# A two-layer decoder trunk on one Trainium2 core: a running sum moved into PSUM, a mask moved to VectorE, and a new order of the work

## The chip, the core and the metric

The kernel runs on one core of a Trainium2 chip. The core has four engines that compute: TensorE (PE in the profile; the loading of its stationary operand is shown apart, as PEld), VectorE (DVE), ScalarE (ACT) and GpSimd (POOL). SyncE (SP) only starts transfers. Each engine runs its own instructions in the order in which they were written, and waits on semaphores for the others. SBUF is the working memory of 128 partitions, PSUM the memory that TensorE writes to, in banks of 512 f32 columns.

The metric is the time of one execution on the device in microseconds, lower is better. A time of a kernel is the median of its runs.

## What is computed

Two layers with 256 positions and 1024 channels. Each layer runs four sub-layers, each between two RMS norms:

```
x += 0.5 * post(swiglu(pre(x)))     # FFN, 2816 hidden channels
x +=       post(mixer(pre(x)))      # layer 0: mLSTM, layer 1: attention
x += 0.5 * post(swiglu(pre(x)))     # second FFN
x +=       post((p @ w_ple) * sigmoid(pre(x) @ w_gate))
```

In the attention of layer 1 there are 8 heads with two score matrices each; a score matrix is masked so that a query sees no later key, its row maximum is subtracted, and the exponentials are summed:

```
s = q @ k.T;  s = where(key_pos <= query_pos, s, -inf);  a = softmax(s)
diff = a[:, :, 0] - lam * a[:, :, 1];  o = diff @ v
```

## The kernel before

**Tiles.** The 256 positions are two tiles of 128 (t is 0 or 1). A product with f32 accuracy is made of three TensorE passes: every operand is split into a rounded part (`whi`, `xh`, `hh`: ScalarE copies it) and the rest (`wlo`, `xl`, `hl`: VectorE subtracts), and hi·hi, hi·lo and lo·hi are added in PSUM (`mm3`, line 610). So each weight block of 128 partitions x 2048 columns passes through a DMA into a `wraw` buffer, a 2048-wide ScalarE copy and a 2048-wide VectorE subtraction before TensorE can use it.

**PSUM.** There are three banks `accI` for products with input weights, four `accO` for the sums of the output projections and one `tr` for transposes.

**Block pairs.** Two neighbouring blocks of 512 FFN columns are computed together (`block_pair`, line 821) by a scheme that takes seven products of half blocks where eight would do it plainly. A product is 12 matmuls of 512 columns (`times`, line 866). The scheme needs sums and differences of weights (`wraw` + `wraw`, made by VectorE, or by a DMA that adds, which POOL starts) and of inputs (`forms`, line 803). Its first lines are the ones that change:

```
ax, ay = acc_in(), acc_in()
times(ax, quarter(0, 0), w11, False)
p1 = held(ax)                                     # ScalarE copies the bank to SBUF
times(ay, quarter(0, 4), w21, False)
nc.vector.tensor_tensor(p1, ay, p1, op=ALU.add)   # VectorE adds the two products
use(0, 0, p1)
```

After these lines `ax` goes on being summed up by the next product of the scheme, so the copy `p1` is needed. The FFNs have 19 block pairs, the mLSTM two more. `hidden` (line 921) takes the result `p1` through SiLU and a multiplication and transposes it for the output projection (`stage_out`, line 940).

**End of a sub-layer.** `post` (line 703) takes the squares of the sum (ScalarE), adds them (POOL), takes the power of -0.5 (POOL), and VectorE adds the scaled result to `x`. `pre` (line 785) transposes `x` on TensorE in two halves, multiplies by a gain (VectorE, `att<-tr,gcol`) and splits the result into `xh` (ScalarE) and `xl` (VectorE), the inputs of the next products.

**Attention.** `weights` (line 1349) puts the mask into two PSUM banks with a matmul (identity times a mask tile, line 1355), adds the scores onto it with matmuls of 64 rows, and VectorE takes the maximum of a whole bank (line 1368). ScalarE then takes the exponentials from PSUM.

**The last step.** `ple` (line 1044) ends the kernel: for the second tile it works on pieces of 512, 256 and 256 columns, takes the squares of each on ScalarE, adds three sums on POOL, and takes the power.

**The order of the work.** No instruction stands where the code writes it. `trunk` only records operations; a planner (`Notes.play`, line 350) plays them through with a cost for each (`cost`, line 258) and for transfers (`step`, `later`, lines 400 to 414), picks at each moment an operation for an engine that is free, and so sets the order of each engine and the buffers. TensorE takes the ready operation of lowest rank, the others the one that is due first (`backward`, line 311). Three tables written out by hand then bend the plan: `FIRST` (this operation before that), `SHIFT` (change when an operation is due) and `MOVE` (change the rank of matmuls). `SLACK` and `LATE` are times added to the landing of an adding and of a plain transfer. What the planner thinks of costs has no part in the run: only the order it writes does.

Of the kernel before, what the change touches and what calls it, by code (L numbers as in the profile page):

```python
# [33 lines left out]
)  # L34
SHIFT = (
# [16 lines left out]
)  # L52
MOVE = (
# [12 lines left out]
)  # L66
SLACK = 3000
LATE = 1000
LANES = 8
# [15 lines left out]
LOCAL = {(0, 0, 3)}  # L85

# [1541 lines left out]
```

## Time and profile before

| what | value |
|---|---|
| median of 3 runs | 991.07 us (989.76 to 994.2) |
| the profiled execution's own time | 990.61 us |
| its span, first to last instruction | 988.8 us |
| TensorE busy | 977.0 us, 99% of the span |
| VectorE busy | 896.0 us, 91% |
| ScalarE busy | 714.7 us, 72% |
| GpSimd busy | 99.7 us, 10% |
| transfers | 274.70 MB, mean 278 GB/s |

A row of the timeline gives the start, the duration, the engine, the operation as `out<-in` with buffer numbers left out, its shape, a count, and in brackets the idle time of that engine just before and what ended it. Matmuls overlap one another, so the pace of TensorE is read from the distance of starts and not from durations. A row of the waits gives who waited for whom, the sum, the number of times and the longest. All lines read L536 in before, because one line writes out every recorded operation; groups are told apart by tiles.

### The profile page before, as it was taken

The page shows a single profiled execution, that of the slowest core. Times are in us where ns is not written, and L with a number is a line of the kernel's source. Part 1 is how long each engine was busy: PE and PEld are TensorE (multiplying, and loading weights), DVE is VectorE, ACT ScalarE, POOL GpSimd, SP SyncE. Part 2 cuts the span into 40 slices and gives each one's busy share as a digit, 9 for nine tenths or more (in the row PEclk, how much of TensorE's full clock was granted, in tenths as well). Part 3 has the DMA queues.
Part 4 walks back from the last instruction along what each step waited for, and adds up shares of the span by engine and source line. Part 5 has one row for each costly group of instructions (what it writes and reads, how often), then busy time and mean ns, then how long its engine had stood idle before and what let it go on. Part 6 is the DMA issues. An engine that isn't in the chain of part 4 may idle for free. (4 is left out here: it accounts for less than half of the span.)

```text
span 988.8 us, 12411 instructions
## 1 busy us (share of the span) xinstructions
PE 977.0 (99%) x4598; PEld 798.9 (81%) x4598; DVE 896.0 (91%) x898; ACT 714.7 (72%) x954; POOL 99.7 (10%) x133
## 2 busy tenths in 40 slices
PE   9999999999999999999999999999999999999997
PEld 7878888887777888888888888888888888888886
DVE  6999999789999999998799999898975999999983
ACT  7668767678867776776777777686775777867763
POOL 0000000300140000001120000001102320000010
PEclk9999999999999999999999999999999999999999
DMA  9999956966799999775699999854668799995721
GB/s 356 414 313 350 286 218 256 304 215 221 288 312 296 328 339 318 292 272 205 258 299 336 334 353 350 325 217 192 216 253 259 214 340 346 305 287 229 284 86 43
DMA packets 45862, 274.70 MB, mean 278 GB/s; under 512 B 5481, under 2 KB 5865, under 8 KB 16105
## 3 DMA queue, kind: packets, MB, share of 16 engines
q1 hardware_dynamic: 39752, 231.69, 60.1%
q0 software_dynamic: 5760, 41.95, 20.9%
q8 instruction: 36, 0.59, 0.2%
q10 hardware_dynamic: 288, 0.27, 0.1%
q14 instruction: 26, 0.20, 0.1%
HBM read 263.40 MB, written 10.49 MB: 277 GB/s over the span
## 5 line engine op out<-in xcount | busy, mean ns | idle before, releaser
L536 DVE TENSOR_TENSOR wraw<-wraw,wraw 128x2048 f32<-128x2048 f32 x44 | 100.5, 2283 | 0.1
L536 ACT ACTIVATE whi_0r<-wraw 128x2048 fp32r<-128x2048 f32 (+2 forms) x49 | 79.5, 1633 | 12.7 <-DVE wraw L536 4.7
L536 ACT ACTIVATE whi_2r<-wraw 128x2048 fp32r<-128x2048 f32 (+1 forms) x49 | 77.8, 1599 | 12.5 <-PE accI L536 8.1
L536 ACT ACTIVATE whi_1r<-wraw 128x2048 fp32r<-128x2048 f32 (+2 forms) x50 | 77.7, 1567 | 8.4 <-DVE wraw L536 4.0
L536 ACT ACTIVATE att<-accI 128x512 f32<-128x512 f32 x84 | 49.7, 593 | 44.6 <-PE accI L536 44.0
L536 ACT ACTIVATE whi_3r<-wraw 128x2048 fp32r<-128x2048 f32 (+1 forms) x46 | 74.2, 1616 | 10.4 <-PE accI L536 4.4
L536 ACT ACTIVATE whi_5r<-wraw 128x2048 fp32r<-128x2048 f32 (+1 forms) x46 | 77.3, 1688 | 5.9 <-PE accI L536 3.3
L536 ACT ACTIVATE whi_4r<-wraw 128x2048 fp32r<-128x2048 f32 (+1 forms) x45 | 73.5, 1645 | 8.3 <-PE accI L536 5.2
L536 POOL DMA_DIRECT2D wraw<-in_ffn_in x36 | 32.0, 889 | 335.2 <-DMA wraw<-in_ffn_in 203.6
L536 POOL TENSOR_SCALAR sm<-sm 128x1 f32<-128x1 f32 x32 | 29.1, 909 | 287.2 <-ACT sg L536 281.7
L536 ACT ACTIVATE sg<-att,sm 128x256 f32<-128x256 f32 x57 | 28.4, 502 | 18.7 <-DVE att L536 17.9
L536 POOL TENSOR_TENSOR sm<-sm,mhalf 128x1 f32<-128x1 f32 (+2 forms) x40 | 28.9, 722 | 101.5 <-DVE sm L536 98.9
L536 ACT ACTIVATE sg<-accO 128x512 bf16<-128x512 f32 (+2 forms) x46 | 20.4, 450 | 21.2 <-PE accO L536 15.6
L536 PEld LDWEIGHTS tr<-ident,sg 128*128 128x128 f32 x176 | 23.4, 140 | 13.4 <-DVE hl_0r L536 1.7
L536 PE MATMUL tr<-ident,sg 128*128 128x128 f32 x176 | 33.8, 273 | 0.1
L536 DVE SCALAR_TENSOR_TENSOR wraw<-wraw,sm,wraw 128x512 f32<-128x512 f32 x32 | 22.6, 748 | 10.4 <-POOL sm L536 10.4
L536 DVE TENSOR_TENSOR wlo_0r<-wraw,whi_1r 128x2048 fp32r<-128x2048 f32 (+1 forms) x13 | 25.3, 1955 | 3.8 <-PE accI L536 3.5
L536 DVE TENSOR_TENSOR att<-accI,att 128x512 f32<-128x512 f32 x42 | 28.3, 682 | 0.0
L536 ACT ACTIVATE att<-accI,sm 128x512 f32<-128x512 f32 (+1 forms) x22 | 14.7, 668 | 17.2 <-PE accI L536 17.1
L536 DVE SCALAR_TENSOR_TENSOR sg<-att,sm,sg 128x256 f32<-128x256 f32 x57 | 26.8, 479 | 0.1
L536 ACT ACTIVATE hh_2r<-tr 128x256 fp32r<-128x256 f32 x30 | 11.3, 378 | 21.2 <-PE tr L536 10.1
L536 DVE TENSOR_TENSOR wlo_2r<-wraw,whi_0r 128x2048 fp32r<-128x2048 f32 (+1 forms) x12 | 25.2, 2108 | 1.4 <-ACT whi_0r L536 1.1
(610 smaller groups left out, 3242.5 us busy)
## 6 DMA issues: line engine op xcount, KB each, us to landing
wraw<-in_ffn_in SPq DMA_DIRECT2D x102, 1024.0 KB, 8.8
wraw<-in_ffn_out SPq DMA_DIRECT2D x44, 1024.0 KB, 10.1
wraw<-in_ffn_in POOLq DMA_DIRECT2D x36, 1024.0 KB, 13.4
wraw<-in_mlstm_in SPq DMA_DIRECT2D x14, 1024.0 KB, 6.4
wraw<-in_ple_gate SPq DMA_DIRECT2D x8, 1024.0 KB, 5.5
wraw<-in_w_kv SPq DMA_DIRECT2D x8, 1024.0 KB, 4.9
home<-wraw SPq DMA_DIRECT2D x28, 256.0 KB, 3.5
wraw<-home SPq DMA_DIRECT2D x14, 512.0 KB, 4.4
```

Of the source, the lines that this page charges most:

```text
L536: getattr(getattr(self.nc, eng), name)(*args, **kw)
```

## The change

Four things are changed, in code that also gets options which stay off here (`PAIRED` is empty, `cut` is never used).

First, in 16 block pairs (four of each of the four FFNs; a pair that an FFN begins with is left as it was) ScalarE copies the first product from one PSUM bank to another, and the second product is added onto that copy by TensorE. VectorE's addition goes away, and the result is read from PSUM.

Second, in attention the mask matmuls go. VectorE adds the mask and takes the minimum of the negated sums in one operation for each score tile (128 or 256 columns), writes the tile to SBUF, and ScalarE takes the exponentials from there.

Third, the squares of the last tile of the kernel are summed by VectorE in a chain of three operations that ends in the whole sum, so that POOL takes only the power.

Fourth, the planner's rates and landing times of transfers are changed, and all three tables are new. This gives another order on every engine.

The transposes are written as matmuls with the transpose flag, of which only the first of four opens the bank. `MODES` with "vvvv" for one pair stands for what `LOCAL` said before.

```diff
-SLACK = 3000
-LATE = 1000
+SLACK = 900
+LATE = 900
...
-    (4319, 4321), (4319, 4385), (5365, 5244), (5365, 5188), (2092, 2061), (5251, 5220), (5057, 5062), (5222, 5423),
+    (4307, 4309), (1810, 1812), (1476, 1543), (2450, 2447), (2068, 1983), (5058, 5225), (453, 514), (1960, 1981),
...
-                o.lat = size / 199.0
+                o.lat = size / 217.0
...
-                o.lat = size / (270.0 if slow else 423.0) + 100
+                o.lat = size / (346.0 if slow else 428.0) + 100
...
-                share = {k: 1.0 if len(act) == 1 else (0.38, 0.62)[k] for k in act}
+                share = {k: 1.0 if len(act) == 1 else (0.31, 0.69)[k] for k in act}
...
-            t += 810 + SLACK if q.kw.get("accum_op") is not None else 180 + LATE
+            t += 1960 + SLACK if q.kw.get("accum_op") is not None else 655 + LATE
...
-                flow[adds].append([s + (2780 if adds else 2160), o.lat, o])
+                flow[adds].append([s + (3405 if adds else 2310), o.lat, o])
...
-            nc.tensor.transpose(pt[:, i * P:(i + 1) * P], src[:, k * P:(k + 1) * P], ident)
+            nc.tensor.matmul(pt[:, i * P:(i + 1) * P], src[:, k * P:(k + 1) * P], ident, start=i == 0, stop=i == 3,
+                             is_transpose=True)
...
-        p1 = held(ax)
-        times(ay, quarter(0, 4), w21, False)
-        nc.vector.tensor_tensor(p1, ay, p1, op=ALU.add)
+        if fork:
+            nc.scalar.activation(ay, ax, AF.Copy)
+            times(ay, quarter(0, 4), w21, True)
+            p1 = ay
+        else:
+            p1 = held(ax)
+            times(ay, quarter(0, 4), w21, False)
+            nc.vector.tensor_tensor(p1, ay, p1, op=ALU.add)
...
-            squares(sg, 1.0, s2[t], i)
+            if epilogue is None and t == NT - 1:
+                v = small()
+                nc.vector.tensor_tensor_reduce(waste(c1 - c0), sg, sg, 1.0 / 1024, EPS if i == 0 else vs[-1], ALU.mult, ALU.add, v)
+                vs.append(v)
+            else:
+                squares(sg, 1.0, s2[t], i)
             nc.vector.tensor_tensor(hg[:, c], sg, gbc[:, c], op=ALU.mult)
...
-            r = rnorm(s2[t], n, 1.0)
+            r = rpow(vs[-1]) if epilogue is None and t == NT - 1 else rnorm(s2[t], n, 1.0)
...
-            for j in range(2):
-                nc.tensor.matmul(pv[j][:, :, L - P:], ident_r, mask_b.unsqueeze(1).to_broadcast([P, ng, P]), start=True, stop=False)
...
-                            kT[hd // 4][rows, hd % 4, c], start=False, stop=i == ng - 1 and kt == t)
+                            kT[hd // 4][rows, hd % 4, c], start=i == 0 and kt == 0, stop=i == ng - 1 and kt == t)
...
-                nc.vector.tensor_reduce(nm[:, :ng], pv[j], axis=AX.X, op=ALU.max, negate=True)
...
-                    nc.scalar.activation(e[:, i, :], pv[j][:, i, :], AF.Exp, bias=nm[:, i:i + 1],
+                    nc.vector.tensor_tensor_reduce(e[:, i, :], pv[j][:, i, :], mask[:, S - L:], -1.0, 3.0e38,
+                                                   ALU.add, ALU.min, nm[:, i:i + 1])
+                    nc.scalar.activation(e[:, i, :], e[:, i, :], AF.Exp, scale=-1.0, bias=nm[:, i:i + 1],
                                          accum_out=zz[:, i:i + 1])
```

The order is shown at three places, with rows as they stand on an engine. In these rows `accI_0_90` is the first of the three input banks, `accO_2_95` an output bank, `tr_0_97` the transpose bank; the numbers tell buffers apart.

The first place is the border from the first FFN of layer 1 to attention, where TensorE transposes the new `x` of the first tile (`wraw`) and then needs `xh` and `xl` made from it. TensorE before:

```order
L536 MATMUL tr_0_97<-ident_0_129,wraw_0_76 128x128 x4
L536 MATMUL accO_2_95<-whi_5r_70,hl_1r_124 128x512
L536 MATMUL accI_1_91<-ident_0_129,wraw_0_76 128x128 x4
L536 MATMUL accO_3_96<-wlo_4r_75,hh_1r_121 128x512
L536 MATMUL accO_3_96<-whi_5r_70,hl_1r_124 128x512
L536 MATMUL accO_3_96<-whi_5r_70,hh_1r_121 128x512
L536 MATMUL accO_3_96<-wlo_4r_75,hh_1r_121 128x512
L536 MATMUL accO_3_96<-whi_5r_70,hl_1r_124 128x512
L536 MATMUL accI_0_90<-whi_2r_67,xh_6r_112 128x512
L536 MATMUL accI_0_90<-wlo_1r_72,xh_6r_112 128x512
L536 MATMUL accI_0_90<-whi_2r_67,xl_6r_119 128x512
```

TensorE after, at the same place:

```order
L547 MATMUL accO_0_93<-wlo_0r_71,hh_2r_122 128x512
L547 MATMUL accO_1_94<-wlo_0r_71,hh_2r_122 128x512
L547 MATMUL accO_0_93<-whi_3r_68,hl_2r_125 128x512
L547 MATMUL accO_1_94<-whi_3r_68,hl_2r_125 128x512
L547 MATMUL tr_0_97<-ident_0_129,wraw_1_77 128x128 x4
L547 MATMUL accI_0_90<-whi_2r_67,xh_6r_112 128x512
L547 MATMUL accI_0_90<-wlo_1r_72,xh_6r_112 128x512
L547 MATMUL accI_0_90<-whi_2r_67,xl_6r_119 128x512
```

Before, six output matmuls and the transposes of the other half stand between the transposes and the product that needs them; after, none do, and the transposes of the other half stand 11 output matmuls further up. On VectorE, from the new `x` of the first tile to its first splits, stands before:

```order
L536 SCALAR_TENSOR_TENSOR wraw_0_76<-wraw_7_83,sm1_7_163,wraw_0_76 128x512 x2
L536 TENSOR_TENSOR att_2_100<-tr_0_97,gcol_0_130 128x512
L536 TENSOR_TENSOR wraw_7_83<-accO_2_95,wraw_7_83 128x512
L536 TENSOR_TENSOR xl_6r_119<-att_2_100,xh_6r_112 128x512
L536 TENSOR_TENSOR att_0_98<-accI_1_91,gcol_0_130 128x512
```

Between the new `x` and `xl` stand the gain and one other operation. On VectorE at the same place stands after:

```order
L547 SCALAR_TENSOR_TENSOR wraw_1_77<-wraw_9_85,sm1_7_163,wraw_1_77 128x512 x2
L547 TENSOR_TENSOR wlo_4r_75<-wraw_5_81,whi_0r_65 128x2048
L547 TENSOR_TENSOR wlo_2r_73<-wraw_6_82,whi_5r_70 128x2048
L547 TENSOR_TENSOR att_4_102<-tr_0_97,gcol_0_130 128x512
L547 TENSOR_TENSOR wraw_9_85<-accO_1_94,wraw_9_85 128x512
L547 TENSOR_TENSOR wraw_9_85<-accO_0_93,wraw_9_85 128x512
L547 TENSOR_TENSOR xl_6r_119<-att_4_102,xh_6r_112 128x512
L547 TENSOR_TENSOR att_1_99<-accI_2_92,gcol_0_130 128x512
L547 TENSOR_TENSOR wlo_0r_71<-wraw_2_78,whi_1r_66 128x2048
L547 TENSOR_TENSOR xl_1r_114<-att_1_99,xh_1r_107 128x512
```

Two 2048-wide weight splits now stand between the new `x` and the gain, and two additions where one stood between the gain and `xl`.

The second place is the first changed block pair of the second FFN of layer 1: the end of the first product and the begin of the second. TensorE before:

```order
L536 MATMUL accI_0_90<-whi_5r_70,xh_0r_106 128x512
L536 MATMUL accI_0_90<-wlo_0r_71,xh_0r_106 128x512
L536 MATMUL accI_0_90<-whi_5r_70,xl_0r_113 128x512
L536 MATMUL accI_2_92<-whi_4r_69,xh_4r_110 128x512
L536 MATMUL accI_2_92<-wlo_3r_74,xh_4r_110 128x512
```

The second product follows the first at once, in a bank of its own. On TensorE at this place stands after:

```order
L547 MATMUL accI_1_91<-whi_3r_68,xh_0r_106 128x512
L547 MATMUL accI_1_91<-wlo_3r_74,xh_0r_106 128x512
L547 MATMUL accI_1_91<-whi_3r_68,xl_0r_113 128x512
L547 MATMUL accI_0_90<-whi_5r_70,xh_4r_110 128x512
L547 MATMUL accI_0_90<-wlo_0r_71,xh_4r_110 128x512
```

The rows stand alike, but after, `accI_0_90` is the copy that ScalarE takes of `accI_1_91`, and nothing stands between. Of the 16 changed pairs this is the only one with nothing between; seven have four 512-column matmuls there, two have five, one has six, and the others ten or more.

The third place is early in the second FFN of layer 0: `hidden` transposes a block (`sg`), ScalarE takes it as `hh`, and the output projection uses it. TensorE before:

```order
L536 MATMUL tr_0_97<-ident_0_129,sg_2_128 128x128 x2
L536 MATMUL accI_2_92<-wlo_0r_71,xh_3r_109 128x512
L536 MATMUL accI_2_92<-whi_0r_65,xl_3r_116 128x512
L536 MATMUL accI_2_92<-whi_0r_65,xh_3r_109 128x512
L536 MATMUL accO_2_95<-whi_3r_68,hh_2r_122 128x512
```

Three matmuls stand between the transposes and the first use of `hh`. On TensorE at this place stands after:

```order
L547 MATMUL accI_0_90<-whi_3r_68,xl_2r_115 128x512
L547 MATMUL tr_0_97<-ident_0_129,sg_0_126 128x128 x2
L547 MATMUL accO_1_94<-whi_2r_67,hh_1r_121 128x512
L547 MATMUL accO_0_93<-whi_2r_67,hh_1r_121 128x512
L547 MATMUL accO_1_94<-wlo_2r_73,hh_1r_121 128x512
```

The three matmuls between the transposes and their first use are gone.

More of the change, by code (lines that the diff above doesn't have):

```diff
@@ L84, with forked @@
 PAIRS = (3, 5, 7, 9), (1, 3, 5, 7, 9), (1, 3, 5, 7, 9), (1, 3, 5, 7, 9)
-LOCAL = {(0, 0, 3)}
+MODES = {"003": "vvvv"}
+PAIRED = ()
+FORK = ('ffn',)
+LONG = 700
+ROUNDS = 10
+FIRST = (
[3 rows of a table added]
+)
+SHIFT = (
[14 rows of a table added]
+)
+MOVE = (
[20 rows of a table added]
+)
+def forked(*tags):
+    return any(t in FORK for t in tags)
 ENGINES = ("tensor", "scalar", "vector", "gpsimd", "sync")
@@ L800, in pre, with forms_in @@
         return go
+    def forms_in(xfs):
+        a11, a12, a21, a22 = xfs
+        q1, q2, q3, q4 = [quarter_parts() for _ in range(4)]
+        was, nc.is_urgent = nc.is_urgent, False
+        for out, x0, x1, op, q in (
+                (a22, a21, a22, ALU.subtract, q1), (a21, a11, a21, ALU.subtract, q3),
+                (a11, a22, a11, ALU.subtract, q2), (a12, a12, a11, ALU.add, q4)):
+            nc.vector.tensor_tensor(out, x0, x1, op=op)
+            split(*q, out)
+        nc.is_urgent = was
+        return [q1, q2, q3, q4]
     def forms(xfs, keep=False, urgent=False):
@@ L815, in forms, with block_pair @@
         return [q1, q2, q3, q4]
-    def block_pair(xts, xf, src, src2, use, end=False, between=None, nxt=None, ahead=None, local=False):
+    def block_pair(xts, xf, src, src2, use, end=False, between=None, nxt=None, ahead=None, mode="ddvv", cut=False, fork=False):
         def load(src, plus=None):
@@ L846, in block_pair @@
         w21 = parts(b21)
-        if local:
+        if by3 == "v":
             b22 = load(src2[1])
@@ L904, in block_pair @@
         use(1, 1, z5)
+        if cut:
+            for i, c in enumerate((slice(0, 256), slice(256, 512))):
+                times(ax, quarter(1, 4), wt4, True, c)
+                use(0, 1, ax, c)
+            return ahead
         times(ax, quarter(1, 4), wt4, True)
@@ L994, in both, with mode_of @@
         def both(item, **kw):
-            return block_pair(xts, all_forms, win[item[0]], win[item[1]], lambda b, t, src: hidden(item[b], t, src),
-                              local=is_local(item), **kw)
-        def is_local(item):
-            return (l, f, item[0]) in LOCAL
+            return block_pair(xts, all_forms, win[item[0]], win[item[1]], lambda b, t, src: hidden(item[b], t, src), fork=forked(f'f{l}{f}{item[0]}', 'first' if item == items[begin] else 'ffn'), **kw)
+        def mode_of(item):
+            return MODES.get(f"{l}{f}{item[0]}", "ddvv")
         ahead = None
@@ L1004, in ffn @@
                 nxt = items[begin + n + 1]
-                ahead = both(item, between=late if split_begin and n == 0 else None, ahead=ahead,
-                             nxt=[win[i] for i in nxt] + [is_local(nxt)] if len(nxt) == 2 else None)
+                ahead = both(item, between=late if split_begin and n == 0 else None, ahead=ahead, mode=mode_of(item),
+                             nxt=[win[i] for i in nxt] + [mode_of(nxt)] if len(nxt) == 2 else None)
             else:
@@ L1028, in ffn @@
         else:
-            both(item, end=True, ahead=ahead)
+            both(item, end=True, ahead=ahead, mode=mode_of(item))
             for t in range(NT):
@@ L1059, in ple @@
         res = []
-        s2 = [small(4) for _ in range(NT)]
+        s2 = [small(4) for _ in range(1 if epilogue is None else NT)]
         left = [2, 2]
@@ L1075, in end, with gated @@
                 res.append(epilogue(t))
+        if xfs is not None:
+            done = [0, 0]
+            def gated(b, t, src, c=slice(0, 512)):
+                gate(t, b, c.start, c.stop, src[:, c], done[t])
+                done[t] += 1
+                if c.stop == 512:
+                    left[t] -= 1
+                if not left[t]:
+                    end(t, done[t])
+            block_pair(xts, lambda: forms(xfs, urgent=True), a["ple_gate"][l, 0], a["ple_gate"][l, 1], gated, end=True, mode=MODES.get(f"ple{l}", "ddvv"), fork=forked(f"ple{l}"), cut=epilogue is None)
+            return res
         ws = [in_weights(a["ple_gate"][l, nb], m=2) for nb in range(2)]
@@ L1115, in mlstm @@
         qT, kT = qkT
-        ws = [in_weights(a["mlstm_in"][b]) for b in range(2)]
+        if "qk" not in PAIRED:
+            ws = [in_weights(a["mlstm_in"][b]) for b in range(2)]
         bg = T([HA, 2], "bg", 1)
@@ new lines, in diff_attn, with room, valued @@
+        if "v" in PAIRED:
+            uts = [None, None]
+            gw = []
+            def room(t):
+                if uts[t] is None:
+                    uts[t] = new_xt()
+                return uts[t]
+            def valued(b, t, src):
+                nc.scalar.activation(v[t][:, b * 512:(b + 1) * 512], src, AF.Copy, scale=kv_rs[t])
+                if (b, t) == (1, 1):
+                    return
+                if t == 0:
+                    heads(0, 4 * b, w0[b], on[0])
+                    to_xt4(on[0], 4 * b, room(0), sub)
+                else:
+                    gw.append(load_gbc(a["norm_g"][l, 3]))
+                    gw.append(out_weights(a["diff_out"], m=2))
+                    for b in range(2):
+                        for g in (2 * b, 2 * b + 1):
+                            heads(1, 2 * g, w1[g], on[1])
+                        to_xt4(on[1], 4 * b, room(1), sub)
+            v.extend(pair(D))
+            block_pair(vxts, lambda: forms_in(vraws), a["w_kv"][2], a["w_kv"][3], valued, end=True, mode=MODES.get("v", "ddvv"), fork=forked("v"))
+            gbc, ws = gw
+        else:
+            uts = [new_xt(), new_xt()]
+            for b in range(2):
+                value(0, b)
+                heads(0, 4 * b, w0[b], on[0])
+                to_xt4(on[0], 4 * b, uts[0], sub)
+            gbc = load_gbc(a["norm_g"][l, 3])
+            ws = out_weights(a["diff_out"], m=2)
+            for b in range(2):
+                value(1, b)
+                for g in (2 * b, 2 * b + 1):
+                    heads(1, 2 * g, w1[g], on[1])
+                to_xt4(on[1], 4 * b, uts[1], sub)
```

121 lines of the change are left out of this document (66 added, 55 removed), and 67 rows, old and new, of tables (FIRST, MOVE, SHIFT).

## The prediction

> **What bounds the kernel now.** I read the page first. TensorE is busy almost without a break, at the full granted clock.
>
> ```profile
> span 988.8 us, 12411 instructions
> PE 977.0 (99%) x4598; PEld 798.9 (81%) x4598; DVE 896.0 (91%) x898; ACT 714.7 (72%) x954; POOL 99.7 (10%) x133
> ...
> PEclk9999999999999999999999999999999999999999
> ```
>
> The execution took 990.6 us, so 1.8 us lie around the span. A busy share can hide waiting, so next come the waits of TensorE, all of them:
>
> ```profile
> PE tr L536 <- DVE wraw L536: 1.1, 1, 1.1
> PE tr L536 <- DVE sg L536: 1.0, 1, 1.0
> PE accI L536 <- ACT att L536: 0.7, 1, 0.7
> PE accI L536 <- DVE wlo_1r L536: 0.7, 1, 0.7
> PE accI L536 <- ACT whi_1r L536: 0.5, 1, 0.5
> PE accI L536 <- DVE wlo_0r L536: 0.2, 1, 0.2
> ```
>
> In 989 us TensorE waits six times, 4.2 us in all. So the time is the number of matmuls by their pace, these waits, and the end after the last matmul. VectorE is at 91%, but a microsecond taken from it is worth nothing where nobody waits for it. The question is then which matmuls go, and where the new order makes TensorE wait.
>
> **The end.** The timeline after the last matmul shows a chain through all engines:
>
> ```profile
> 981.78 0.47 ACT L536 ACTIVATE att<-accI,sm 128x256 f32<-128x256 f32 x1 [1.40 <-PE accI L536]
> 982.29 0.42 DVE L536 TENSOR_TENSOR att<-accO,att 128x256 f32<-128x256 f32 x1 [1.99 <-ACT att L536]
> 982.75 0.42 ACT L536 ACTIVATE sg<-att 128x256 bf16<-128x256 f32 x1 [0.49 <-DVE att L536]
> 982.75 0.42 DVE L536 TENSOR_TENSOR wraw<-att,wraw 128x256 f32<-128x256 f32 x1
> 983.07 0.19 ACT L536 ACTIVATION_READ_ACCUMULATOR sg<-att 128x1 f32 x1
> 983.42 0.29 POOL L536 TENSOR_SCALAR sm<-sm,sm 128x1 f32<-128x1 f32 x1 [2.64 <-ACT sg L536]
> 983.79 0.56 POOL L536 TENSOR_TENSOR sm<-sm,mhalf 128x1 f32<-128x1 f32 x1
> ```
>
> Between VectorE's product and the power lie 1.04 us (982.75 to 983.79): the squares, the reading of the sum, POOL's addition. The new reduction runs on VectorE; its bounds are 0.42 (a 256-wide operation) and 0.61 (with a reading such as ScalarE's 0.19), so the power may start 0.4 us earlier. But the multiplication of 0.42 us now runs beside the power, and this trace shows what VectorE can do to POOL:
>
> ```profile
> 290.55 4.21 POOL L536 TENSOR_SCALAR sm<-sm 128x1 f32<-128x1 f32 x1 [7.14 <-ACT sg L536]
> ```
>
> An addition of one column that takes 0.29 us at the end took 4.21 us in the middle, while VectorE ran 2048-wide additions. If the power waits for the multiplication, the gain is 0. I take 0.3, bounds 0 and 0.4. [...]
>
> **The mask.** Twelve matmuls go: eight of 256 columns, four of 512.
>
> ```profile
> L536 PE MATMUL accO<-hl_0r,hh_2r 128*128 128x256 f32 x8 | 2.0, 290 | 0.0
> 713.00 0.62 PE L536 MATMUL accO<-hl_0r,hh_2r 128*128 128x512 f32 x2
> 713.46 0.39 PE L536 MATMUL accI<-whi_3r,xh_5r 128*128 128x512 f32 x1
> ```
>
> Two of 512 columns take 0.46 us of TensorE's pace, 0.23 each; one of 256 half, 0.115. That is 4 x 0.23 + 8 x 0.115 = 1.84 us; with a little of the 0.29 us duration around them up to 2.3. I take 1.9.
>
> VectorE gets 16 operations of 128 columns and 16 of 256 for twelve reductions.
>
> ```profile
> 702.85 0.68 DVE L536 TENSOR_REDUCE sm<-accO 128x4 f32<-128x512 f32 x1
> 709.30 0.35 DVE L536 SCALAR_TENSOR_TENSOR att<-att,sm,att 128x128 f32<-128x128 f32 x1
> 713.07 0.49 DVE L536 SCALAR_TENSOR_TENSOR att<-att,sm,att 128x256 f32<-128x256 f32 x1
> 700.00:725.00 25.00, 25.00 (x169) 20.38 (x169) 22.71 (x40) 20.21 (x62) 0.00 (x0) 1.00 0.60 225
> 725.00:750.00 25.00, 25.00 (x147) 21.11 (x144) 19.00 (x36) 19.45 (x50) 2.99 (x3) 1.00 0.68 260
> ```
>
> The nearest rows give 16 x 0.35 + 16 x 0.49 = 13.4 us against 12 x 0.68 = 8.2. The operation is written as two instructions, the second one column wide; such small ones stand at up to 0.19 us (ScalarE's reading), 32 of them up to 6 us. So VectorE does 5 to 11 us more where these two windows leave 2.3 and 6.0 us free. Weight splits can slide, so TensorE feels little; 0.5 us, bounds 0 and 2.
>
> **The copy in PSUM.** VectorE loses 16 additions of 0.68 us, 11 us, behind which nobody waited: worth 0. ScalarE's copy stays a copy of 512 columns. New is that TensorE may not begin the second product before it. This wait exists in the trace, once, in the mLSTM, where two products follow each other in one bank:
>
> ```profile
> L536 ACT ACTIVATE att<-accI 128x512 f32<-128x512 f32 x84 | 49.7, 593 | 44.6 <-PE accI L536 44.0
> 249.72 0.39 PE L536 MATMUL accI<-whi_4r,xl_3r 128*128 128x512 f32 x1
> 250.21 0.60 ACT L536 ACTIVATE att<-accI 128x512 f32<-128x512 f32 x1
> 250.86 0.50 PE L536 MATMUL accI<-whi_0r,xh_5r 128*128 128x512 f32 x1 [0.75 <-ACT att L536]
> ```
>
> From the last matmul to the next start lie 1.14 us, 0.91 more than the pace. So a copy is hidden by four matmuls of 0.23, if ScalarE is free. By the order one pair has no cover: 0.91 and some 0.1 to get going again, 1.0. Ten have four to six: I take 0.07 each, 0.7; if ScalarE comes 0.3 us late at each, 3. Five are covered well: 0.
>
> **The order: what leaves.** Three of the six waits (0.7 for `att`, 0.7 and 0.5 for weights) lie in the mLSTM. The wait for `att` had no matmul between; now another bank's product stands there. Of these 1.9 us I take 1.5 as gained, bounds 0.5 and 1.9. The wait of 1.1 us for `x` hangs on the slow POOL addition above; I leave it in, and count its loss only in the lower end.
>
> **The order: what comes.** At the border to attention, the chain from the transposes to the first product that needs them, before:
>
> ```profile
> 688.25 0.60 PE L536 MATMUL tr<-ident,wraw 128*128 128x128 f32 x4
> 688.46 0.61 ACT L536 ACTIVATE sg<-wraw 128x512 bf16<-128x512 f32 x1
> 689.62 0.63 ACT L536 ACTIVATE xh_6r<-att 128x512 fp32r<-128x512 f32 x1 [0.45 <-DVE att L536]
> 690.28 0.69 DVE L536 TENSOR_TENSOR xl_6r<-att,xh_6r 128x512 fp32r<-128x512 f32 x1
> 690.52 0.39 PE L536 MATMUL accI<-whi_2r,xh_6r 128*128 128x512 f32 x1
> 677.29 2.28 DVE L536 TENSOR_TENSOR wlo_2r<-wraw,whi_1r 128x2048 fp32r<-128x2048 f32 x1
> 251.73 1.91 ACT L536 ACTIVATE whi_1r<-wraw 128x2048 fp32r<-128x2048 f32 x1
> ```
>
> From the transposes to the end of `xh` are 2.0 us (688.25 to 690.25), all of it under the six output matmuls and other transposes. After, nothing stands there: a wait of 2.0 - 0.36 = 1.6 us at least. Two weight splits of 2.28 us stand ahead of the gain on VectorE, the second behind a ScalarE split of 1.91 that follows two squares of 0.61, of which the first runs on the first half of `x`. Counted from the whole new `x`, VectorE comes free at 0.61 + 1.91 + 2.28 and 0.1 between, 4.9; TensorE ends its transposes at about 0.4 + 0.36 + 11 x 0.23 + 0.36 = 3.65 (0.4 from `x` to the first transposes is my estimate from this place before). The gain (as wide as the 0.69 of `xl`) and the copy of 0.63 follow: a wait of 4.9 + 1.3 - 3.65 = 2.5. Then `xl` stands behind two additions: 3 x 0.69 = 2.1 after the gain, against 0.63 + 2 x 0.23 = 1.1 of TensorE: 1.0. The next half's `xl` stands behind gain and another split: 0.69 + 2.28 + 0.69 = 3.7 against twelve matmuls, 2.8: 0.9. Together 4.4; rows of VectorE overlap by some 0.1 each, so I take 4.0, bounds 1.6 and 5.0.
>
> In the second FFN of layer 0 an output projection now stands right behind its transposes:
>
> ```profile
> 310.63 0.38 PE L536 MATMUL tr<-ident,sg 128*128 128x128 f32 x2
> 311.55 0.67 PE L536 MATMUL accO<-whi_3r,hh_2r 128*128 128x512 f32 x2
> ```
>
> The 0.92 us held two transposes and three matmuls; without those three TensorE waits 3 x 0.23 = 0.7, bounds 0 and 1.0.
>
> **The sum.** 990.6 - 1.9 (mask) - 0.3 (end) - 1.5 (mLSTM) + 0.5 (mask on VectorE) + 1.0 + 0.7 (copies) + 4.0 (border) + 0.7 (projection) = 993.8 us. The profiled execution lies 0.5 us under the median of 991.07 and inside the spread of the three runs; I add nothing for that. All lower ends: 990.6 - 2.3 - 0.4 - 1.9 - 1.1 + 0.9 + 1.6 = 987.4. All upper ends: 990.6 - 1.9 - 0.5 + 2 + 1.0 + 3 + 5.0 + 1.0 = 1000.2.
>
> **Rivals.** A measurement of this kernel can tell about 0.5%, 5 us: the edges are 986.1 and 996.0.
>
> *The border costs nothing.* If VectorE and ScalarE have their weight splits done early there, so that every wait the order shows is short, the lower sum falls by the remaining 1.6 and 0.9 to about 985: faster. For it: VectorE loses 11 us of additions, so it may run ahead. Against: the chain of transposes, gain and copy has a length of its own, and nothing is left beside it. Chance 0.16, of which 0.12 under 986.1.
>
> *Nothing comes of it.* The new waits turn up as small ones, gains and losses cancel: 990.6, within 0.5%. Chance 0.11.
>
> *ScalarE is late with the copies, slower.* In ScalarE's order a 2048-wide weight split stands directly ahead of 14 of the 16 copies. A copy is late when that split starts less than 1.91 us before the product's end. If it is so at half of the eleven close ones, by half a split, 5 x 0.95 = 4.7 us come on top: 998.5. Against it: 84 such copies had ScalarE idle for 44.0 us ahead of them, 0.5 us each, so ScalarE mostly stands ready. An adding transfer of 1 MB that lands late would work the same way: by the numbers of the diff the planner now counts on it after 3405 + 1960 + 900 + 1048576/217 = 11,100 ns instead of 2780 + 810 + 3000 + 1048576/199 = 11,860. Chance 0.13.
>
> *The clock drops, slower.* The trace shows the granted clock fall only after the end:
>
> ```profile
> 984.00:986.00 2.00, 0.00 (x0) 0.00 (x0) 1.41 (x2) 0.00 (x0) 0.35 (x1) 0.78 0.00 1
> 986.00:988.80 2.80, 0.00 (x0) 0.00 (x0) 0.00 (x0) 0.00 (x0) 0.00 (x0) 0.50 0.50 187
> ```
>
> The last stretch is at half clock, so 0.78 means 0.88 us of the two at half: it fell at 985.1, 3.4 us after the last matmul ended at 981.8, while waits of 1.1 us left it alone. The border's first wait, 2.5 us, stays below that; if it grew past 3.4, about 3.4 us at half clock would lose 1.7 us, with the longer wait 996.4. Chance 0.05. [...]
>
> **How the numbers follow.** The forecast has 0.55: 0.45 within 0.5%, 0.10 above 996.0. With the rivals: faster 0.12, same 0.45 + 0.04 + 0.11 = 0.60, slower 0.10 + 0.13 + 0.05 = 0.28. The range runs from 986.0, which takes in a part of the first rival, to 1000.0, the upper sum; some 0.17 lie outside.
>
> **What would show it.** In the profile after: TensorE's waits sum to about 9.5 us instead of 4.2; the largest is at the border, for `xh` and `xl`, with about 4 us; one wait of 0.8 to 1.0 us for ScalarE's write to `accI` stands early in the last FFN, and the other copies show waits under 0.2. Twelve matmuls fewer. The power at the end starts within 1.1 us of VectorE's last gate product. The prediction is wrong if the border shows no wait, if copies other than that one wait for ScalarE by more than 0.5 us each, or if a transfer shows up among TensorE's releasers.

## The result, and the profile after

The changed kernel takes 994.82 us (median of 11 runs, 994.12 to 995.7), the kernel before 990.57 us beside it (989.5 to 994.2): a ratio of 1.004, 95% interval 1.0033 to 1.0048. It is slower by 4.2 us, less than the 0.5% that the prediction set as "no change", and 1.0 us above the forecast. The profiled execution took 994.82 us itself.

The page after, the lines that answer to the first fence of the prediction:

```profile
span 993.0 us, 12425 instructions
...
PE 979.8 (99%) x4586; PEld 797.3 (80%) x4586; DVE 890.9 (90%) x938; ACT 712.1 (72%) x948; POOL 101.1 (10%) x131
```

The twelve matmuls are gone (4598 to 4586), and the span is 4.2 us longer all the same. The page can't say why: TensorE is at 99% in both. The waits of TensorE after (total, times, longest; five of 0.2 to 0.4 us, one of them for `xl_6r`, are left out):

```profile
PE accI L547 <- ACT xh_6r L547: 2.0, 1, 2.0
PE tr L547 <- DVE sg L547: 1.0, 1, 1.0
PE tr L547 <- DVE hl_0r L547: 0.7, 1, 0.7
PE accI L547 <- ACT accI L547: 0.7, 1, 0.7
PE accO L547 <- ACT hh_1r L547: 0.5, 1, 0.5
...
```

All together they sum to 6.2 us, not 9.5. The forecast waits are all there: the border (`xh_6r`, then `xl_6r`), one copy (`accI` for ScalarE's write to `accI`), the projection (`hh_1r`). But 2 us more of wait and 12 matmuls less do not make 4.2 us more. What a list of waits hides is seen in TensorE's timeline at the border, and in the stretches of 2 us around it (busy time of PE, PEld, DVE, ACT and POOL, then PEclk, DMA share and GB/s):

```profile
690.30 0.60 PE L547 MATMUL tr<-ident,wraw 128*128 128x128 f32 x4
692.91 0.51 PE L547 MATMUL accI<-whi_2r,xh_6r 128*128 128x512 f32 x1 [2.02 <-ACT xh_6r L547]
...
694.05 0.79 PE L547 MATMUL accI<-whi_2r,xl_6r 128*128 128x512 f32 x1 [0.19 <-DVE xl_6r L547]
694.64 0.63 PE L547 MATMUL accI<-whi_2r,xh_6r 128*128 128x512 f32 x1
695.07 0.63 PE L547 MATMUL accI<-wlo_1r,xh_6r 128*128 128x512 f32 x1
...
696.97 0.39 PE L547 MATMUL accI<-whi_2r,xh_6r 128*128 128x512 f32 x1
690.00:692.00 2.00, 0.90 (x7) 0.53 (x5) 2.00 (x2) 1.65 (x3) 0.00 (x0) 1.00 0.00 0
692.00:694.00 2.00, 0.94 (x2) 0.30 (x2) 2.00 (x5) 1.74 (x4) 0.32 (x1) 0.82 0.66 168
694.00:696.00 2.00, 1.95 (x5) 1.57 (x6) 2.00 (x2) 1.90 (x2) 2.00 (x4) 0.50 0.84 356
696.00:698.00 2.00, 2.00 (x9) 1.62 (x8) 2.00 (x3) 0.00 (x0) 0.95 (x1) 0.83 0.24 33
```

From 694.64 on nothing waits, yet the matmuls stand 0.43 us apart instead of 0.23: TensorE runs at half clock (0.50 in the row 694.00:696.00). The share at half in the three lower stretches is 0.72, 2.00 and 0.68 us (a mean of 0.82 is 36% at half), together 3.4 us, from 693.28 to 696.68.

So the waits are the wrong count. The right one is the time that TensorE loses against its own pace: in its timeline, the distance from one row to the next, less 0.227 us for each 512-column matmul of the row, 0.115 for 256 and 0.055 for 128 columns (constants, which cancel between kernels: the first two are near the 0.23 and 0.12 us at which rows of 512 and 256 columns stand apart in these traces where nothing waits, the third, an estimate, is about a quarter of the first; a gap of just one matmul is a missing record and left out). Summed by stretch of the span, in us, with two experiments that are told below:

| stretch | before | before's order, mask and last squares (e5) | after | border entry out (e1) |
|---|---|---|---|---|
| 0 to 30 | 4.9 | 5.2 | 5.7 | 5.9 |
| 30 to 200, first FFN | 5.2 | 5.2 | 5.2 | 5.2 |
| 200 to 300, mLSTM | 10.9 | 10.3 | 7.5 | 7.5 |
| 300 to 350, second FFN begins | 0.8 | 0.8 | 3.1 | 3.1 |
| 350 to 660 | 9.1 | 10.4 | 9.8 | 9.6 |
| 660 to 700, border | 2.2 | 2.2 | 6.0 | 3.0 |
| 700 to 790, attention | 9.6 | 9.7 | 9.9 | 11.8 |
| 790 to the last matmul | 5.1 | 5.0 | 7.1 | 6.4 |

Between kernels of the same order a cell differs by up to 0.7 us, in one case (350 to 660) by 1.3. The border costs 3.8 us and the second FFN 2.3; the mLSTM gives 3.4 back.

The tail after, VectorE and POOL:

```profile
986.80 0.42 DVE L547 TENSOR_TENSOR att<-accO,att 128x256 f32<-128x256 f32 x1 [1.58 <-ACT att L547]
...
987.66 0.42 DVE L547 TENSOR_TENSOR wraw<-att,wraw 128x256 f32<-128x256 f32 x1
987.83 0.67 POOL L547 TENSOR_TENSOR sm<-sm,mhalf 128x1 f32<-128x1 f32 x1 [9.51 <-DVE sm L547]
```

The power starts 1.03 us after the start of VectorE's last gate product; before, it was 1.50 (982.29 to 983.79).

### The profile page after: what moved, and what is told of

It reads as the page before. It is cut to its first block, busy times and chain, and to the rows that moved or that the text cites. A ratio compares the mean times of both kernels' runs of the same rounds, so it can differ in the third digit from the quotient of the medians.

```text
span 993.0 us, 12425 instructions
## 1 busy us (share of the span) xinstructions
PE 979.8 (99%) x4586; PEld 797.3 (80%) x4586; DVE 890.9 (90%) x938; ACT 712.1 (72%) x948; POOL 101.1 (10%) x131
## 4 chain that ended last, share of the span: by engine, by line
PE 84%; DVE 5%; issue 5%; POOL 3%; ACT 2%; DMA 1%; SPq 0%; POOLq 0%; DVEq 0%; ACTq 0%
PE accI L547 52%; PE accO L547 28%; PE tr L547 4%; POOL sm L547 3%; DVE wraw L547 2%; ACT sg L547 1%; DMA wraw<-in_x 1%; DVE wlo_4r L547 1%; DMA wraw<-in_xT 1%; DVE att L547 0%; DVE wlo_0r L547 0%; DVE wlo_2r L547 0%; DVE wlo_1r L547 0%; ACT att L547 0%; DVE wlo_3r L547 0%
## 5 line engine op out<-in xcount | busy, mean ns | idle before, releaser
L547 ACT ACTIVATE whi_3r<-wraw 128x2048 fp32r<-128x2048 f32 (+1 forms) x49 | 81.5, 1668 | 11.0 <-PE accI L547 9.9
L547 ACT ACTIVATE whi_2r<-wraw 128x2048 fp32r<-128x2048 f32 (+1 forms) x46 | 73.9, 1620 | 14.7 <-PE accI L547 10.8
L547 ACT ACTIVATE whi_1r<-wraw 128x2048 fp32r<-128x2048 f32 (+2 forms) x46 | 73.8, 1615 | 8.9 <-DVE wraw L547 5.9
L547 ACT ACTIVATE att<-accI 128x512 f32<-128x512 f32 x68 | 40.4, 595 | 22.0 <-PE accI L547 21.2
L547 ACT ACTIVATE sg<-accI,sm 128x256 f32<-128x256 f32 x47 | 21.8, 467 | 17.5 <-PE tr L547 11.6
L547 ACT ACTIVATE sg<-wraw 128x512 bf16<-128x512 f32 x32 | 20.0, 625 | 10.1 <-DVE wraw L547 8.7
L547 ACT ACTIVATE sg<-att,sm 128x256 f32<-128x256 f32 x41 | 20.5, 502 | 9.2 <-DVE att L547 9.1
L547 ACT ACTIVATE hh_1r<-tr 128x256 fp32r<-128x256 f32 x29 | 11.0, 380 | 21.3 <-PE accO L547 11.1
L547 DVE SCALAR_TENSOR_TENSOR sg<-accI,sm,sg 128x256 f32<-128x256 f32 x47 | 22.4, 477 | 3.1 <-ACT sg L547 3.1
L547 DVE TENSOR_TENSOR att<-att,att 128x512 f32<-128x512 f32 (+1 forms) x35 | 23.3, 667 | 1.1 <-ACT att L547 1.1
```

The source lines that it names most:

```text
L547: getattr(getattr(self.nc, eng), name)(*args, **kw)
```

## The experiments

**One part alone, in the order of before.** Four kernels leave the order of the work as it was: the old plan is made first, then the changed program is recorded and its operations are tied to the old places.

```diff
+def keep_order(old, new):
+    at = {(o.eng, o.key): i for i, o in enumerate(old.sched)}
...
+        for p, o in zip(here, here[1:]):
+            o.after.setdefault(p, False)
```

The mask, with the lines of the change and nothing else of it:

```diff
-            for j in range(2):
-                nc.tensor.matmul(pv[j][:, :, L - P:], ident_r, mask_b...
-                nc.vector.tensor_reduce(nm[:, :ng], pv[j], axis=AX.X, op=ALU.max, negate=True)
+                    nc.vector.tensor_tensor_reduce(e[:, i, :], pv[j][:, i, :], mask[:, S - L:], -1.0, 3.0e38,
+                                                   ALU.add, ALU.min, nm[:, i:i + 1])
```

> The kernel before, every engine's order kept, with the mask and the maximum on VectorE alone. Theory, the terms of the prediction: 12 matmuls less, 1.9 us, and 0.5 us back because VectorE does 5 to 11 us more: 1.4 us less than the kernel before, about 989.2. Rival: the attention waits for VectorE now: between 0 and 2 us more than before, with new waits of TensorE's transposes for VectorE or ScalarE between 700 and 775 us.

Measured: 989.81 against 990.77 us, ratio 0.999 (0.9982 to 0.9999). The order being the same, the two traces can be laid on each other matmul by matmul. Behind the attention a matmul stands so, in the kernel with the mask on VectorE and in the one before:

```profile
779.00 0.39 PE L539 MATMUL accI<-whi_2r,xl_0r 128*128 128x512 f32 x1
```
```profile
780.35 0.39 PE L536 MATMUL accI<-whi_2r,xl_0r 128*128 128x512 f32 x1
```

That is 1.35 us earlier; at 679 us it is 0.03, and all of the 1.35 comes between there and 729. The sum of the two terms, -1.9 and +0.5, is shown; how it divides between them is not. VectorE's price, here and in the kernel before:

```profile
L539 DVE CUSTOM_DVE_ANT_0 att<-accO,sg 128x128 f32<-128x128 f32 (+1 forms) x32 | 9.2, 354 | 0.2 <-PE accO L539 0.2
L539 DVE DVE_READ_ACCUMULATOR2_ANT sm<- 128x1 f32 x32 | 2.7, 85 | 0.0
```
```profile
L536 DVE TENSOR_REDUCE sm<-accO 128x2 f32<-128x512 f32 (+1 forms) x12 | 7.5, 683 | 1.4 <-PE accO L536 1.4
```

By durations that is 32 x (0.354 + 0.085) = 14.0 us against 12 x 0.683 = 8.2: 5.8 more, at the low end of the 5 to 11. But neighbouring instructions overlap: by busy time it is 11.9 against 7.5, 4.4 more.

The last squares alone:

```diff
+                nc.vector.tensor_tensor_reduce(waste(c1 - c0), sg, sg, 1.0 / 1024, EPS if i == 0 else vs[-1], ALU.mult, ALU.add, v)
```

> The kernel before, every engine's order kept, with only the last three squares and their sum on VectorE (no ScalarE squares, no two additions on POOL at the very end). Theory: the power starts within 1.1 us of VectorE's last gate product and the end comes 0.3 us earlier (0 to 0.4), too little for the times alone; the stretch from the last matmul to the end of the span says it. Rival: VectorE's three longer instructions eat it up: 0, or up to 0.3 us more.

Measured: 990.48 against 990.77 us, ratio 0.9993 (0.9985 to 1.0001), which alone would say nothing. From the start of the last matmul to the end of the span it is 7.0 us (980.94 to 987.9) against 7.3 (981.47 to 988.8), and the chain of the end reads as in the changed kernel. The theory holds, by one trace of each kernel.

Both together:

> The kernel before, every engine's order kept, with mask and maximum on VectorE and the last three squares on VectorE, and no copy in PSUM. Theory: the two gains add up (1.35 us between 680 and 730 us in the trace of the mask alone, 0.35 us in the tail of the other): 1.7 us less than before, about 989.0 us, faster than both kernels, so that everything the change loses comes from the order and the copies. Rival: the slot that the mask holds for the whole attention, or VectorE's longer instructions, cost it back together: 0 to 0.5 us less.

Measured: 989.83 against 991.43 us, ratio 0.9983 (0.9974 to 0.9992), 1.6 us faster. The gains add up. This version beats both kernels, and it has neither the copies in PSUM nor the new order; the two together cost the changed kernel about 5.6 us (1.004 against 0.9983).

**The copies alone, in the order of before:**

```diff
-            p1 = held(ax)
-            times(ay, quarter(0, 4), w21, False)
-            nc.vector.tensor_tensor(p1, ay, p1, op=ALU.add)
+            nc.scalar.activation(ay, ax, AF.Copy)
+            times(ay, quarter(0, 4), w21, True)
+            p1 = ay
```

> The kernel before, every engine's order kept, with only the second product of the 16 block pairs accumulating on ScalarE's copy of the first. In this order no matmul lies between the two products at 14 of the 16 places and one at the other two. Theory: each copy costs TensorE 0.9 us, 14.6 us together, and more where ScalarE is inside a weight split of 1.9 us when the product ends: 14 to 22 us more than before, 1005 to 1012 us, as waits of TensorE for ScalarE's write to accI. Rival: VectorE, rid of 11 us of additions, runs ahead and gives it back, or the copies hide: under 5 us more.

Measured: 1015.48 against 990.77 us, ratio 1.0248 (1.0233 to 1.0263): 24.7 us, more than I expected. The row of TensorE's waits for it, and the worst place (ScalarE, TensorE, and the stretches behind it):

```profile
PE accI L539 <- ACT accI L539: 18.5, 16, 2.8
```
```profile
836.70 1.90 ACT L539 ACTIVATE whi_2r<-wraw 128x2048 fp32r<-128x2048 f32 x1
838.49 0.59 ACT L539 ACTIVATE accI<-accI 128x512 f32<-128x512 f32 x1
...
839.13 0.50 PE L539 MATMUL accI<-whi_4r,xh_4r 128*128 128x512 f32 x1 [2.84 <-ACT accI L539]
...
840.00:842.00 2.00, 2.00 (x7) 1.51 (x6) 2.00 (x2) 0.64 (x1) 0.00 (x0) 0.51 1.09 299
842.00:844.00 2.00, 2.00 (x7) 1.63 (x6) 2.00 (x2) 0.64 (x2) 0.00 (x0) 0.64 0.92 348
```

The copy itself is short (0.59 us). But when the product ended, at 836.3, ScalarE was inside one weight split (834.89 to 836.80), and the next one, the 1.90 of the row, stands ahead of the copy in its order. Eight of the sixteen copies found ScalarE ready and cost 0.83 us each; the other eight cost 1.5 to 3.0, 14.3 us in all. With 0.11 us at the first matmul behind each wait (1.8), and 1.7 lost at half clock behind the worst place, that is 24.4 us. So the mechanism of the rival "ScalarE is late with the copies" is real in this order, at half of the places; in the changed kernel, where four or more matmuls stand in between at 15 of 16 places, it did not bite.

**The copies undone, in the order of after.** The mirror image: the copy goes to SBUF, and VectorE's addition comes back behind each second product.

> The changed kernel, every engine's order kept, with the copy in PSUM undone in all 16 pairs: the copy goes to SBUF, the second product does not wait, and VectorE adds the two (16 additions of 0.68 us come back, each right behind its second product). Theory: the copies cost 0.8 us at the uncovered place and little at the fifteen others, and VectorE's 11 us are hidden: 0.8 to 1.5 us less than the changed kernel. Rival: the freed VectorE time is what this order lives on: 1 us more or worse, with new waits of TensorE for VectorE in the FFNs.

Measured: 1022.81 against 991.43 us, ratio 1.0318 (1.0303 to 1.0332): both theories miss. Three waits of 3.5 to 7.7 us carry 16.6 of the 28 us. At the longest, TensorE waits for ScalarE, and ScalarE for a transfer, which SyncE issues late (its queue, then ScalarE; and the first of these loads in the changed kernel):

```profile
676.40 0.33 SPq L547 DMA_DIRECT2D att<-in_diff_lambda  x1
676.82 0.38 SPq L547 DMA_DIRECT2D wraw<-in_ffn_out  x1
...
684.30 1.06 ACT L547 ACTIVATE whi_3r<-wraw 128x1024 fp32r<-128x1024 f32 x1 [7.92 <-DMA wraw<-in_ffn_out]
```
```profile
637.91 0.33 SPq L547 DMA_DIRECT2D att<-in_diff_lambda  x1
```

A small load into an `att` buffer stands on SyncE ahead of the next weights, and here it is issued 38 us later, where this kernel as a whole is 12.7 us behind. SyncE waits 32.3 us for it, until ScalarE has read a sum out of an `att` buffer (`sg<-att`, 675.87 to 676.37). The copy in SBUF holds an `att` buffer that the copy in PSUM left free, so that load, and the weights behind it, come late. The run says nothing on the price of a copy. It says what the copy in PSUM also does, which the prediction did not list: it frees a buffer, and the order of SyncE's queue is built on that. In the first FFN, where no such load stands, the matmuls fall behind by 2.7 us from 21 to 162 us; VectorE's four additions of 0.68 are 2.7. There the rival fits.

**The uncovered copy:**

```diff
+    (5208, 5, 52),
```

> The changed kernel with one entry more in MOVE, (5208, 5, 52): five matmuls of the product before stand between the two products of the one pair whose copy had nothing beside it. Theory: the wait of 0.7 us there (0.83 over the pace) shrinks to 0 to 0.4, since ScalarE may still be inside a weight split; 0.4 to 0.8 us less. Rival: the copy starts as much later as the matmuls that stand ahead of it: the same time, with the wait still 0.7.

Measured: 994.64 us, ratio 1.0032 (1.002 to 1.0045) to before; the interval overlaps that of the changed kernel, so the times can't tell. At the place, in the changed kernel and then here:

```profile
822.94 0.50 PE L547 MATMUL accI<-whi_5r,xh_4r 128*128 128x512 f32 x1 [0.67 <-ACT accI L547]
```
```profile
822.00 0.39 PE L547 MATMUL accI<-whi_4r,xl_1r 128*128 128x512 f32 x1
822.43 0.50 PE L547 MATMUL accI<-whi_5r,xh_4r 128*128 128x512 f32 x1
```

The loss falls from 0.83 to 0.20 us here, and some 0.5 of the gain is still there at 850 us. By the trace the theory holds, at its lower end.

**The border.** First the one table entry that sends the transposes of the first half of `x` behind the whole projection:

```diff
-    (4304, 1, 350),
```

> The changed kernel, with one entry of its table MOVE taken out: (4304, 1, 350), which sends the four transposes of the first half of x at the border to attention to the very end of the output projection. Theory: the three waits at the border (2.39, 0.57 and 0.36 us over the pace in the trace) fill with matmuls, and with them goes the half clock of about 3 us behind them (some 1.0 us lost over five matmuls). New small waits are allowed, 1 us in all. Sum 3.3 + 1.0 - 1.0: 2.5 to 4 us less than the changed kernel, 991 to 992 us, and a granted clock of 1.00 between 690 and 700 us. Rival one: the wait only moves, to the next half's copy or to the attention's own products: 0 to 1 us less. Rival two: the half clock has nothing to do with the wait and stays: 2 us less, clock again 0.8 somewhere near 695 us.

Measured: 992.78 us, ratio 1.0019 (1.001 to 1.0028) to before: 2.0 us less than the changed kernel. No half clock shows at the border: the matmuls from 694.75 to 696.11 us stand 0.23 us apart, and the mean granted clock of the execution is 0.998 (0.997 in the changed kernel). The border loses 3.0 us instead of 6.0. But the attention's order, which the planner makes anew, loses 1.9 us more. So the theory holds at the border, the first rival behind it, and the whole falls short of the 2.5 to 4 us.

Then the transposes alone are moved on TensorE, and every other engine keeps its order:

```diff
+            here.remove(plan.ops[4304])
+            here.insert(here.index(plan.ops[4308]), plan.ops[4304])
```

> The changed kernel, every engine's order kept, but on TensorE the border's last four transposes moved to where the kernel before had them, some 2.9 us earlier, ahead of the other half's. Theory: the gain on VectorE stands behind two weight splits of 2.28 us, the second of which ends after the transposes even now; so the first product starts within 0.3 us of where it did, TensorE's wait is longer by what the transposes took, and the time is the same (0 to 0.3 us less). Rival: the late transposes alone make the wait: 2 us less or more.

Measured: 995.07 us, ratio 1.0044 (1.003 to 1.0057). The transposes now start at 687.46, and yet:

```profile
693.07 0.50 PE L547 MATMUL accI<-whi_2r,xh_6r 128*128 128x512 f32 x1 [2.05 <-ACT xh_6r L547]
692.00:694.00 2.00, 0.83 (x2) 0.30 (x2) 2.00 (x4) 1.59 (x4) 0.18 (x1) 0.89 0.52 139
694.00:696.00 2.00, 1.80 (x4) 1.49 (x5) 2.00 (x3) 2.00 (x2) 2.00 (x4) 0.50 0.92 385
696.00:698.00 2.00, 2.00 (x8) 1.56 (x7) 2.00 (x3) 0.05 (x1) 1.09 (x1) 0.76 0.10 12
```

The product starts where it did. The late transposes are what the order shows, but not what the product waits for: that is VectorE's gain behind a weight split that ends at 691.6 (changed kernel):

```profile
689.31 2.29 DVE L547 TENSOR_TENSOR wlo_2r<-wraw,whi_5r 128x2048 fp32r<-128x2048 f32 x1 [0.46 <-ACT whi_5r L547]
691.52 0.68 DVE L547 TENSOR_TENSOR att<-tr,gcol 128x512 f32<-128x512 f32 x1
```

So the steps on VectorE and ScalarE are moved too:

```diff
+        for i, by in ((4304, 0), (4305, 1), (4306, 1), (4307, 2), (4310, 1), (4311, 1)):
```

> The run before, and besides the steps behind those transposes moved: VectorE's gain ahead of the second weight split, ScalarE's copy ahead of the square, VectorE's xl ahead of two additions, and the next half's copy and xl ahead of one weight split each. Theory: the gain ends at 689.5, the copy (behind a ScalarE split that ends at 691.1) at 691.7, so the first product starts some 1.1 us earlier, xl no longer waits, and the clock stays at full: 2 to 3 us less than the changed kernel, if the two splits that come 0.6 us later are not waited for. Rival: the wait goes over to the second half's xl or to the splits: under 1 us less.

Measured: 994.39 us, ratio 1.0037 (1.0025 to 1.005). My theory falls here. The first product starts at 691.77, the clock stays at 1.00, the second half begins at 694.95 (697.66 in the changed kernel): 2.7 us won, and 2.1 of them lost again at the transposes of the second token tile:

```profile
691.77 0.51 PE L547 MATMUL accI<-whi_2r,xh_6r 128*128 128x512 f32 x1 [0.78 <-ACT xh_6r L547]
694.95 0.51 PE L547 MATMUL accI<-whi_4r,xh_1r 128*128 128x512 f32 x1
698.64 0.66 PE L547 MATMUL tr<-ident,wraw 128*128 128x128 f32 x4 [1.53 <-DVE wraw L547]
```

VectorE is busy for 9.3 of the 10 us from 690 to 700, so what one step gains the next one pays. This fits a border that costs because VectorE and ScalarE have weight splits and the norm of both tiles to do while TensorE has no projection left, and not because of one late step; where projection was left (the run with the table entry out), the border lost half as much.

**The clock.** TensorE is kept busy in the border's wait by transposes that write the same values into the same bank again, 36 in one kernel and 16 in the other; nothing else is changed.

```diff
+    k = plan.order.index(plan.ops[4304].parts[-1]) + 1
+    plan.order[k:k] = 9 * plan.ops[4308].parts
```

> The changed kernel with 36 more transposes (the second half's group of four, nine times more, into the same bank with the same values) right behind the border's last transposes: TensorE is busy for some 2 us of the border's wait, and nothing else is changed. Theory: the half clock of 693.3 to 696.7 us comes from TensorE standing still, so it goes: granted clock 1.00 from 692 to 698 us, the matmuls from 694 us on at 0.23 us and not 0.43, 0.9 to 1.3 us less than the changed kernel, with the first product starting where it did. Rival: the clock falls for another reason (the power of what runs there, or the time): the half clock stays and the time is the same, or longer if the transposes push the product.

> As the run with 36 transposes, with 16 of them: they take 0.107 us each there, so 1.7 us, which ends before the first product can start. Theory: the first product starts where it did in the changed kernel (2.6 us after the last transposes of x began), at full clock, and the five matmuls that ran at half pace get their 0.2 us each back: 0.8 to 1.2 us less than the changed kernel. Rival: 1.7 us of the wait filled isn't enough and the half clock stays: the same time.

Measured: 995.62 us, ratio 1.0046 (1.0032 to 1.0059), with 36; 994.46 us, ratio 1.0041 (1.0029 to 1.0054), with 16. The timeline with 36 (3.85 us of transposes, longer than the wait), the first and the tenth matmul of the product:

```profile
691.12 4.09 PE L547 MATMUL accI<-ident,wraw 128*128 128x128 f32 x36
694.97 0.48 PE L547 MATMUL accI<-whi_2r,xh_6r 128*128 128x512 f32 x1
...
697.11 0.39 PE L547 MATMUL accI<-whi_2r,xh_6r 128*128 128x512 f32 x1
```

No half clock, in either kernel: with 36 the matmuls from 695.28 us on stand 0.23 us apart, and with 16 the granted clock is 1.00 in each stretch of 2 us from 690 to 700. With 36 the product starts 4.28 us after `x`'s last transposes (690.69), with none 2.61 us, and yet its tenth matmul comes earlier, 6.42 us after them against 6.67. Both kernels miss the forecast of some 1 us less. With 16:

```profile
693.14 0.60 PE L547 MATMUL tr<-ident,wraw 128*128 128x128 f32 x4
695.77 0.50 PE L547 MATMUL accI<-whi_2r,xh_6r 128*128 128x512 f32 x1 [0.28 <-ACT xh_6r L547]
699.29 0.39 PE L547 MATMUL accI<-whi_4r,xh_1r 128*128 128x512 f32 x1
```

The product starts at 2.63 us, as expected, and the second half's first matmul comes 1.2 us sooner (6.15 us behind the transposes against 7.36). But these two runs alone don't show that the transposes kept the clock up. The kernel with the covered copy has the same border and no more transposes; its product waits as long, and its clock stays at 1.00 too:

```profile
693.42 0.50 PE L547 MATMUL accI<-whi_2r,xh_6r 128*128 128x512 f32 x1 [2.00 <-ACT xh_6r L547]
692.00:694.00 2.00, 0.58 (x2) 0.30 (x2) 2.00 (x5) 1.38 (x6) 0.00 (x0) 1.00 0.39 82
```

So half clock followed the wait of 2.02 us in one execution, and none followed the wait of 2.00 us in another; what decides it was not shown.

The time hardly moves: laid on the changed kernel matmul by matmul, only 0.4 of the 1.2 us is left at 705 us, since the next thing late is VectorE's `xl` of the second half (a wait of 0.5). The half clock cost 1.2 us where it ran, and 0.4 behind it. The kernel with the covered copy says the same: laid on the changed one, it wins 1.2 us at the border, and 0.5 are left at 705 us.

## Why the prediction was right, point by point

- **Mask**, -1.9 and +0.5: shown alone, -1.35 together.
- **End**, -0.3: shown alone, 7.3 to 7.0 us. The power started during VectorE's multiplication (987.83 against 987.66) and took 0.67 us instead of 0.56; it did not wait for the multiplication, the case for which I allowed 0. This trace doesn't tell whether the 0.11 comes from VectorE.
- **The uncovered copy**, 1.0: 0.83.
- **Ten close copies**, 0.7: nothing. Weight loads waited for a copy nine times, as the row says, but behind the other fifteen copies no matmul lost time. Four matmuls of 0.227 cover 0.83 us, if ScalarE is free.

```profile
PEld accI L547 <- ACT accI L547: 2.7, 9, 1.1
```

- **Border**, 4.0: 3.8, the right size by another sum. The first wait was 2.5 in the sum; the product lost 2.39. The second and the third were 1.0 and 0.9; TensorE lost 0.57 before `xl`, and nothing at the second half, because by then it had run at half clock and was late itself. In the kernel with the covered copy, at full clock, the third wait is there and loses 0.64.
- **The clock rival** was right that half clock can follow a wait of TensorE, and wrong on the point from which it does: I let it begin with a wait of 3.4 us, read from the end of one trace, and gave it a length of 3.4 us, an estimate that no row of before shows. In the changed kernel it came behind a wait of 2.0 us and lasted 3.40 us, and at the end of that trace the clock falls 4.0 us after the last matmul (986.2 to 990.2).
- **Projection**, 0.7: 0.74 (309.82 to 310.67, less two transposes). But two more losses stand in the same FFN that I had not looked for, 0.37 at 312.0 and, with another cause, 0.51 here:

```profile
330.53 0.39 PE L547 MATMUL accI<-whi_5r,xl_6r 128*128 128x512 f32 x1
331.27 0.50 PE L547 MATMUL accI<-whi_3r,xh_2r 128*128 128x512 f32 x1 [0.35 <-DVE sg L547]
```

  Here a product waits for its bank, until VectorE has read the last part of a block out of it (`sg`). With the copy in PSUM the sum itself is read from the bank, and the bank is held until the gate's product is done; before, VectorE's addition freed it. But the copy is not the cause of the wait: with the copies undone in the same order, the same product waits 0.85 us, for that addition. The new order gives it a bank that is not free yet, which the prediction did not price.
- **mLSTM**, -1.5: -3.4 by the table, of which 0.7 is the variation of one execution, since the three kernels with the order of before have 10.1 to 10.3 there and not 10.9. That leaves 2.7. The kernels with the new order have 7.4 to 7.5, but for one (10.0; the last section). What in the new order gives it was not tried alone.
- **VectorE's 11 us**, 0: not shown. In the order of before nobody waited for them; with the copies undone in the new order, the first FFN falls 2.7 us behind.
- **Not forecast**: a transposition that waits for `hl_0r` at 25.9 us, 0.8; it is in the changed kernel and in those made from it.

Put together by the table and the single runs: -1.4 (mask) - 0.3 (end) - 2.7 (mLSTM) + 0.8 (copy) + 3.8 (border) + 2.3 (second FFN) + 0.8 (start) = 3.3, and the profiled executions differ by 4.2. The 0.9 us left can't be put down to a place: the last stretch of the table has 1.2 more than the copy, but no row there loses more than 0.4, and missing records account for some of it. The forecast came as near as it did because misses cancelled: the mLSTM gained 1.2 us more and the close copies cost 0.7 less, the second FFN and the start cost 2.4 more.

## What to carry to other kernels

When an operation is moved to hide it, ask which engine's queue the whole chain behind it stands in: moving one engine's step changed nothing at the border, and moving all of them moved the wait to the next tile. Price an accumulation on a copied bank by three things: the copy (0.83 us here, if nothing stands between the products), what the copying engine still has to finish first (up to 2.2 us more here), and how long the bank and the buffers are held. And try the parts of a bundle one by one in the old order: two small parts were worth 1.6 us here, and were hidden under copies and a new order that together cost 5.6.

## What the runs showed of the hardware

**Half clock came in stretches of 3.4 us and longer, behind some waits and not behind others.** In the changed kernel (0.72, 2.00 and 0.68 us at half), in the one with the transposes moved (0.44, 2.00 and 0.96) and in the one with the copies (1.96 and 1.44), the stretch at half clock is 3.40 us each time; it came with a wait of 2.02, 2.05 and 2.84 us. With the copies undone, around its three waits of 3.5 to 7.7 us, some 7, 10 and 7 us are at half (means over 25 us of 0.90 and 0.96 from 425 to 475 us, 0.80 from 675 to 700, 0.86 from 950 to 975). The other way round, a wait of 3.07 us left the clock at 1.00 in the kernel with 16 transposes:

```profile
297.04 0.66 PE L547 MATMUL tr<-ident,wraw 128*128 128x128 f32 x4 [3.07 <-DVE wraw L547]
296.00:298.00 2.00, 0.95 (x7) 0.72 (x8) 1.77 (x4) 0.98 (x3) 1.12 (x2) 1.00 1.12 397
```

The wait of 2.00 us at the border with the covered copy left it at 1.00 too. So the length of the wait alone does not decide it here, and no run was made to tell what does.

**A one-column operation on POOL took from 0.56 to 4.36 us at one place of the mLSTM**, and differently from run to run: an addition of 4.36 us (288.49 to 292.85, beside VectorE's operations of 1024 and 2048 columns) and a power of 0.56 in the changed kernel, 2.40 and 2.45 in the kernel with 16 transposes, where TensorE's wait of 3.07 us followed. What makes them long was not tried.
